# The modulation's matrix-vector products in a two-block network: all accumulation on VectorE, with weight buffers of their own

## The chip, the cores and the metric

The kernel is one program on one core of a Trainium2 chip. The metric is the device time of one execution in microseconds (us). Engines are named as in the profile: PE (TensorE, matrix products), DVE (VectorE), ACT (ScalarE), POOL (GpSimd), SP (SyncE, which here issues the weight loads).

## The reference

Two blocks of two layers each on 256 tokens of width 1024. The first block is FFN, a mixer of three attention kinds, FFN. The second block is conditioned: each of its two layers takes six rows of 1024 numbers from a modulation, for two conditions (the latent's and the context's), and shifts, scales and gates with them. Cut to what matters here:

```python
# c, c_ctx: the conditions' vectors [1024]; ada_w: [layers, 1024, 6 * 1024]
mod     = silu(c)     @ ada_w[i] + ada_b[i]    # six rows of 1024: shift, scale, gate, twice
mod_ctx = silu(c_ctx) @ ada_w[i] + ada_b[i]
h = rms_norm(x) * (1 + scale) + shift           # ahead of each mixer and MLP
x = x + gate * f(h)
```

The products with `ada_w` are matrix-vector products: 25 MB of weights for each layer are read once and multiplied by two vectors. They depend on nothing that the first block computes, so they can run beside it.

## The kernel before, in words

**FFN.** `ffn` goes over the 2816 hidden columns in five chunks of 512 and one of 256. For each chunk two products of 256 tokens x 1024 are formed, gate and up (`gemm`); each takes four weight tiles of 128 x 1024 numbers. `wload` (L230) loads a tile to `wraw` by a DMA in SP's queue (L237), casts it to `whi` on ACT (L244) and forms `wlo = wraw - whi` on DVE (L245). PE multiplies with `whi` and `wlo` in three passes (L284 to L286). After the chunk ACT makes `sg`, DVE makes `av` (L466, twice: one for each token tile), PE transposes `av` (L470), and ACT and DVE split the result to `ahi` and `alo` (L472, L473). Then the down product runs over 22 tiles in two halves, and DVE adds it to `x` (`residual`, L443); PE transposes `x` (L363) and DVE makes the low part of the next layer's input (L372).

**Buffers.** `wtile` (L219) hands out weight buffers in turn: four `wraw` of the program and three more in an FFN (`FFN_MORE`), four `whi` and four `wlo` in an FFN.

**The modulation.** `ada` (L969) is background work. For a group of 1024 columns it goes over eight tiles of 128 rows. A step takes the next `wraw` of the same ring that the FFN's tiles use, issues its load on SP (L982), and adds tile times `c` to an accumulator: for the first condition on DVE in one instruction (L991; L993 for the first tile); for the second condition ACT scales the tile into a buffer (L987) and POOL adds this to the second accumulator (L989). After eight steps PE sums over the partitions (L1001) and POOL writes the result to DRAM. The buffers, two accumulators and two for the scaled tile, lie in one tile `hB` (L1546); in the second block's MLP they are `xA0` and `xA1`. There are twelve groups: six of the first layer and two of the second for both conditions, beside the first block's FFNs; four of the second layer for one condition alone, beside the MLP of both conditions.

**What sets the order.** `background` (L196) takes a list of steps and spreads them over so many weight tiles; `tick` runs a step after each tile (T1 to T4 say over how many). That is the order in the code. The order on each engine is then made by a scheduler: it places an instruction when what it waits for is there in its own reckoning, and of several ready ones the one that comes first in the code. An engine runs its instructions strictly in that order, and SP's queue too.

Of the kernel before, what the change touches and what calls it, by code (L numbers as in the profile page):

```python
# [13 lines left out]
AF = mybir.ActivationFunctionType  # L14
# [6 lines left out]
S = 256  # L21
# [7 lines left out]
# background work: steps of the hyena filter, and how many of them go ahead of the modulation's  # L29
HY, W2 = 14, 4  # L30
# column chunk after which the bias strips are made
CB = 4
# after a gated output product (by token tiles): engines of the next weight tiles' parts (1: lo on GpSimd, 2: hi too)
ENG = {2: [0, 1], 4: [0, 1, 1]}
# weight tiles over which background work is spread, and to wait before
T1, T2, T3, T4 = 40, 54, 28, 36
W1, W3, W4 = 0, 4, 8
# columns of a gated output product's second half (by token tiles)
# [5 lines left out]
def consts():  # L44
    """Arrays that depend on shapes alone."""
# [19 lines left out]
    # second block: local attention's band, rope tables  # L65
# [15 lines left out]
    # retention decay: exponents and masks  # L81
# [5 lines left out]
    # long convolution: odd-frequency transform of length 512, filter features  # L87
# [12 lines left out]
class Net:  # L100
# [95 lines left out]
    def background(self, steps, tiles=1, wait=0):  # L196
        """Steps to run beside the next products, spread evenly over so many weight tiles, after some to wait."""
        self.fill, self.rate = steps, len(steps) / tiles
        self.credit = -wait * self.rate

    def tick(self):
        """After each weight tile: now and then a step of background work."""
        self.credit += self.rate
        while self.fill and self.credit >= 1.0:
            self.credit -= 1.0
            self.fill.pop(0)()
# [12 lines left out]
    def wtile(self, name, shape):  # L219
        """A weight buffer: in turn one of the pool's and of those that a phase adds"""  # L220
# [28 lines left out]
    def tiles(self, src, nk, c0, cn):  # L249
        """Plan of a product's weight tiles: (first k tile, k tiles)"""  # L250
        step = 2 if cn > 256 else 4
        return [(k0, min(step, nk - k0)) for k0 in range(0, nk, step)]

    def gemm(self, lhs, nk, src, c0, cn, nt, k_base=0, mid=None, done=None, skew=(False, False), turn=0):
        """Natural form: one accumulator [tok, cn] per token tile. skew: over the first / last weight
        tiles, the first token tiles go ahead of the last. turn: so many k tiles go last."""
# [35 lines left out]
    def gemm_t(self, hT, nk, src, c0, cn, tok, skew=False, whole=False):  # L292
        """Transposed form: accumulators [128 columns, tok] for cn / 128 column tiles. skew: over the
        first weight tiles, the first half of the tokens goes ahead of the second."""
# [10 lines left out]
        while i < len(plan):  # L305
# [14 lines left out]
            for (kt, wh, wl), c, q in order:  # L320
# [3 lines left out]
                # a bank's first product clears it; the first ones of its other parts then overwrite  # L324
# [7 lines left out]
    def rstd(self, ss, n, inv_n, out=None):  # L332
        """(ss / n + eps) ** -0.5"""
# [7 lines left out]
    def row_stats(self, x, ss, i, nt=2, c0=0, cn=512):  # L341
        """Sums of squares of columns c0 .. c0 + cn to ss[:, t, i]"""
# [5 lines left out]
    def row_rstd(self, ss):  # L348
        """rsqrt of the rows' mean squares, from sums of squares of parts [128, t, parts]"""
# [5 lines left out]
    def split_T(self, x, h, w, hi, lo):  # L355
        """hi, lo parts of (x * w)^T, [d, kt, tok], for half h of the columns"""
# [18 lines left out]
    def prep(self, x, w):  # L375
        """Rows' norm: raw rows times the gain, transposed, half by half; their rsqrt at the end."""
# [15 lines left out]
    def prep_mod(self, x, m, tok, kind, xA):  # L392
        """norm(x) * (1 + scale) + shift, transposed: raw rows times the gain half by half; the rest at the end."""
# [55 lines left out]
    def ffn(self, x, pre, wg, wu, wd, nxt, hook):  # L449
        """pre: this layer's rows, ready; nxt: makes the next layer's; hook: other work, after the first columns"""  # L450
# [33 lines left out]
    def bias_strips(self):  # L484
        """R[h, i] = bias of head h at distance 255 - i (or masked), 128 times in DRAM: strip[p, j] = R[h, j - p + 127]."""
# [17 lines left out]
    def strip(self, pool, h0):  # L503
        """Bias of four heads: [tok p, head, j], of distance p + 128 - j."""
# [6 lines left out]
    def head_stats(self, mp, src, n, r):  # L511
        """r[:, t, :n] = rsqrt(mean square) of the n heads in src [128, 2, n * 64]"""
# [11 lines left out]
    def nat(self, mp, w, c0, cn, lhs, r, name):  # L524
        """Columns c0 .. c0 + cn of norm(x) @ w_in, [tok, t, cn]"""
# [7 lines left out]
    def normed_q(self, mp, src, n, gain, name):  # L533
        """q heads (n, natural) -> normalized, transposed [128 (2 heads, d), n / 2, tok]"""
# [15 lines left out]
    def normed_k(self, mp, src, name):  # L550
        """two key heads -> normalized, each twice: [tok, t, g, 2, 64]"""
# [10 lines left out]
    def put_halves(self, dst0, dst1, ps, gain):  # L562
        """upper partitions to dst0, lower to dst1, times gain"""
# [11 lines left out]
    def mixer_tiles(self):  # L575
        """Keys and stick queries, transposed (a head in both halves of the partitions); the merged branches"""
# [11 lines left out]
    def compress(self, mp, kv1, l, out):  # L588
        """Compressed keys into self.KC; compressed values [(g, n) 32, 64] to out. Returns its steps."""
# [16 lines left out]
        # column groups of the array: (parity of j, key or value)  # L606
# [50 lines left out]
    def key_tiles(self, kd, dst, gain):  # L657
        """kd [tok, t, g, 2, 64] -> dst(g) [(2, 64), keys]"""
# [15 lines left out]
    def nsa(self, mp, t, g, qT, strip, sc, vs, vw, vc, gates, yhi, ylo):  # L674
# [5 lines left out]
        # the two heads of a pair: at the same time in the array's row halves, to different banks  # L680
# [66 lines left out]
        # the heads' parities: at the same time in the array's column halves  # L747
# [84 lines left out]
    def softmax_sink(self, S, rows, sink):  # L832
        """exponentials of S in place; returns 1 / (their sums + the sink's)"""
# [120 lines left out]
    def ada_setup(self):  # L954
# [7 lines left out]
        # to sum over the partitions, to row tok  # L962
# [6 lines left out]
    def ada(self, i, grps, bufs):  # L969
        """Columns g * 1024 .. + 1024 of the modulation of layer i, for both conditions, to DRAM, step by step.  # L970
        bufs: makes four buffers [128, 1024]. Of the last layer, the context's mixer takes two kinds only."""
# [4 lines left out]
        def step(g, kt):  # L976
            toks = (0, 1) if i == 0 or g < 2 else (0,)
            if not st:
                st["bufs"] = bufs()
            acc = st["bufs"][0:2]  # L980
            raw = self.wtile("wraw", [128, 1024])
            nc.sync.dma_start(raw, w[kt * 128:kt * 128 + 128, g * 1024:g * 1024 + 1024])  # L982
            for tok in toks:
                c = self.cT[:, tok * 8 + kt:tok * 8 + kt + 1]
                if tok:
                    y = st["bufs"][2 + kt % 2] if kt else acc[1]
                    nc.scalar.activation(y, raw, AF.Copy, scale=c)  # L987
                    if kt:
                        nc.gpsimd.tensor_add(acc[1], acc[1], y)  # L989
                elif kt:  # L990
                    nc.vector.scalar_tensor_tensor(acc[0], raw, c, acc[0], op0=ALU.mult, op1=ALU.add)  # L991
                else:
                    nc.vector.tensor_scalar(acc[0], raw, c, None, op0=ALU.mult)  # L993
            if kt < 7:
                return
            # sums over the partitions: the four column groups at the same time
# [10 lines left out]
        return [lambda g=g, kt=kt: step(g, kt) for g in grps for kt in range(8)]  # L1007

    def mod_columns(self, i):
        """[128 d, tok, kind, kt] of the modulation of layer i, scales with the norms' gains folded in"""  # L1010
# [31 lines left out]
    def sine(self, pool, arg):  # L1042
        """sin(arg) in place, reduced to [-pi, pi] first"""
# [13 lines left out]
    def hyena_filter(self):  # L1057
        """Transform of the filter (with the skip term folded in as lag 0, before its norm) to DRAM; 1 / norm. Step by step."""
# [68 lines left out]
    def even(self, x, ctx, hT, m, new_hT):  # L1127
# [4 lines left out]
        with tc.tile_pool(name="even", bufs=1) as ep:  # L1132
# [6 lines left out]
            # attention: projections, rotations, transposes  # L1139
# [41 lines left out]
            def attend(t):  # L1181
# [4 lines left out]
                for i in range(4):  # L1186
# [37 lines left out]
                    # the pair's heads: at the same time in the array's column halves  # L1224
# [6 lines left out]
            # long convolution  # L1231
# [376 lines left out]
```

## Time and profile before

| | |
|---|---|
| median of 3 runs | 2518.71 us (2515.84 to 2521.52) |
| profiled execution, span | 2524.6 us |
| PE busy | 2430.4 us, 96% |
| DVE busy | 1568.2 us, 62% |
| ACT busy | 1162.0 us, 46% |
| POOL busy | 308.0 us, 12% |
| adds of L989 on POOL | 56 of 2.96 us |

The span runs from the first to the last instruction of one profiled execution; no other time of that execution is recorded, and it lies 0.2% above the median of the runs. Busy shares are averages over stages. A wait belongs to the engine that stood idle, and names the instruction that ended it. PEclk is the clock that TensorE was granted, as a share of its full speed.

### The profile page before, as it was taken

The numbers are of one execution on the slowest core, as the hardware profiler recorded it, in microseconds if no ns is written. First come the engines' busy times: TensorE is split into PE (matmuls) and PEld (weight loads), VectorE is DVE, ScalarE is ACT, GpSimd is POOL, SyncE is SP. The second block draws the span as 40 slices with busy tenths as digits, with TensorE's granted clock in tenths as the row PEclk, the third lists the DMA queues.
The fourth block names the chain that finished last, engine by engine and source line by source line (L and its number), as shares of the span: only waits on it lengthen the run. The fifth ranks groups of instructions, "written<-read, shape, count | busy, mean of one in ns | idle before, by whom it ended". The sixth has DMA issues, their size and how long they took to land. (4 is left out here: it accounts for less than half of the span.)

```text
span 2524.6 us, 31452 instructions
## 1 busy us (share of the span) xinstructions
PE 2430.4 (96%) x11941; PEld 1933.3 (77%) x11941; DVE 1568.2 (62%) x2181; ACT 1162.0 (46%) x1771; POOL 308.0 (12%) x229
## 2 busy tenths in 40 slices
PE   8899999999998999999899999999999999998998
PEld 7777777777777877787687667777787788887996
DVE  5775576676677457767754674654534745655665
ACT  5544655555544455556443342431333433334543
POOL 2330100133123001003300000100000110110000
PEclk9999999999999999999899999999999999999999
DMA  7685545767666564466743121455522433334553
GB/s 245 214 261 171 176 124 159 234 195 228 214 202 208 157 192 148 133 208 202 226 160 117 51 101 50 129 180 177 160 100 84 136 92 111 112 119 150 183 185 133
DMA packets 212351, 405.86 MB, mean 161 GB/s; under 512 B 14830, under 2 KB 48365, under 8 KB 211688
## 3 DMA queue, kind: packets, MB, share of 16 engines
q1 hardware_dynamic: 207416, 391.77, 49.3%
q0 software_dynamic: 3776, 9.38, 1.1%
q10 hardware_dynamic: 1008, 2.70, 0.3%
q8 instruction: 94, 1.54, 0.2%
q14 instruction: 57, 0.47, 0.1%
HBM read 401.48 MB, written 4.67 MB: 161 GB/s over the span
## 5 line engine op out<-in xcount | busy, mean ns | idle before, releaser
L245 DVE TENSOR_TENSOR wlo<-wraw,whi 128x1024 fp32r<-128x1024 f32 (+1 forms) x617 | 812.9, 1324 | 593.7 <-ACT whi L244 589.8
L244 ACT CAST whi<-wraw 128x1024 fp32r<-128x1024 f32 (+1 forms) x622 | 646.4, 1044 | 893.3 <-PE acc L286 666.4
L284 PE MATMUL acc<-whi,hA 128*128 128x512 f32 (+1 forms) x1472 | 570.2, 388 | 1.4 <-ACT whi L244 1.0
L285 PE MATMUL acc<-wlo,hA 128*128 128x512 f32 (+1 forms) x1472 | 566.4, 385 | 3.4 <-DVE wlo L245 3.4
L286 PE MATMUL acc<-whi,hA 128*128 128x512 f32 (+2 forms) x1152 | 441.0, 383 | 0.0
L284 PEld LDWEIGHTS acc<-whi,hA 128*128 128x128 f32 x1472 | 281.0, 191 | 67.4 <-issue 9.3
L285 PEld LDWEIGHTS acc<-wlo,hA 128*128 128x128 f32 x1472 | 280.5, 191 | 60.1 <-DVE wlo L245 7.0
L284 PE MATMUL acc<-whi,ahi 128*128 128x512 f32 x736 | 293.3, 399 | 0.0
L285 PE MATMUL acc<-wlo,ahi 128*128 128x512 f32 x736 | 291.4, 396 | 1.5 <-DVE wlo L245 1.5
L286 PE MATMUL acc<-whi,alo 128*128 128x512 f32 x736 | 291.2, 396 | 0.0
L326 PE MATMUL acc<-hA,whi 128*128 128x512 f32 (+1 forms) x752 | 259.0, 345 | 3.7 <-ACT hA L425 3.0
L327 PE MATMUL acc<-hA,wlo 128*128 128x512 f32 (+1 forms) x752 | 258.4, 344 | 2.4 <-POOL wlo L245 2.4
L328 PE MATMUL acc<-hB,whi 128*128 128x512 f32 (+1 forms) x752 | 257.4, 344 | 0.0
L286 PEld LDWEIGHTS acc<-whi,hA 128*128 128x128 f32 x1152 | 220.5, 191 | 42.7 <-issue 1.3
L989 POOL TENSOR_TENSOR hB<-hB 128x1024 f32<-128x1024 f32 x56 | 165.7, 2959 | 326.9 <-ACT hB L987 308.7
L285 PEld LDWEIGHTS acc<-wlo,ahi 128*128 128x128 f32 x736 | 138.6, 188 | 34.7 <-DVE wlo L245 2.9
L284 PEld LDWEIGHTS acc<-whi,ahi 128*128 128x128 f32 x736 | 138.6, 188 | 34.3 <-issue 2.1
L286 PEld LDWEIGHTS acc<-whi,alo 128*128 128x128 f32 x736 | 138.5, 188 | 32.9
L326 PEld LDWEIGHTS acc<-hA,whi 128*128 128x128 f32 x752 | 142.3, 189 | 24.9 <-ACT hA L425 3.5
L327 PEld LDWEIGHTS acc<-hA,wlo 128*128 128x128 f32 x752 | 142.5, 189 | 23.6 <-issue 3.4
L328 PEld LDWEIGHTS acc<-hB,whi 128*128 128x128 f32 x752 | 142.1, 189 | 19.3 <-issue 1.4
L991 DVE SCALAR_TENSOR_TENSOR hB<-wraw,cT,hB 128x1024 f32<-128x1024 f32 x56 | 98.6, 1760 | 43.9 <-DMA wraw<-in_ada_w_dram 43.7
(422 smaller groups left out, 2745.9 us busy)
## 6 DMA issues: line engine op xcount, KB each, us to landing
wraw<-in_mlp_w_dram SPq DMA_DIRECT2D x128, 512.0 KB, 3.8
wraw<-in_ada_w_dram SPq DMA_DIRECT2D x96, 512.0 KB, 4.0
wraw<-in_ffn_w_gate_dram SPq DMA_DIRECT2D x88, 512.0 KB, 4.3
wraw<-in_ffn_w_up_dram SPq DMA_DIRECT2D x88, 512.0 KB, 4.5
wraw<-in_ffn_w_down_dram SPq DMA_DIRECT2D x88, 512.0 KB, 3.7
wraw<-in_w_in_dram SPq DMA_DIRECT2D x84, 512.0 KB, 3.7
wraw<-in_od_w_in_dram SPq DMA_DIRECT2D x64, 512.0 KB, 3.7
wraw<-in_ev_w_in_dram SPq DMA_DIRECT2D x18, 512.0 KB, 3.7
```

Source lines behind the costliest of these rows:

```text
L244: nc.scalar.copy(hi[sl], raw[sl])
L245: (nc.gpsimd if e & 1 else nc.vector).tensor_sub(lo[sl], raw[sl], hi[sl].bitcast(F32))
L284: nc.tensor.matmul(o, h, wh, start=kt == first, stop=False)
L285: nc.tensor.matmul(o, h, wl, start=False, stop=False)
L286: nc.tensor.matmul(o, l, wh, start=False, stop=kt == end)
L326: nc.tensor.matmul(o, wh[:, cs], xh[:, kt, ts], start=st, stop=False, skip_group_check=skew_or_pair)
L327: nc.tensor.matmul(o, wl[:, cs], xh[:, kt, ts], start=False, stop=False, skip_group_check=skew_or_pair)
L328: nc.tensor.matmul(o, wh[:, cs], xl[:, kt, ts], start=False, stop=en, skip_group_check=skew_or_pair)
L989: nc.gpsimd.tensor_add(acc[1], acc[1], y)
L991: nc.vector.scalar_tensor_tensor(acc[0], raw, c, acc[0], op0=ALU.mult, op1=ALU.add)
```

## The change

`ada` is written anew. Both conditions are accumulated on DVE, one instruction each (L992 in the new numbering; the first tile of the second condition stays with ACT, L994). POOL adds nothing. The weights no longer come through the ring of `wraw`: the two buffers that held scaled tiles are now two weight buffers in turn, in the same tile `hB` (or `xA1`), and a step first issues the load for the step after it (L980). A new first step makes the buffers and issues the first load, so a phase has one step more. T1, the number of weight tiles over which two of the five phases are spread, goes from 40 to 46. The rest of the diff takes away comments.

```diff
-T1, T2, T3, T4 = 40, 54, 28, 36
+T1, T2, T3, T4 = 46, 54, 28, 36
...
-        def step(g, kt):
+        todo = [(g, kt) for g in grps for kt in range(8)]
+
+        def load(n):
+            g, kt = todo[n]
+            nc.sync.dma_start(st["bufs"][2 + n % 2], w[kt * 128:kt * 128 + 128, g * 1024:g * 1024 + 1024])
+
+        def step(n):
+            g, kt = todo[n]
             toks = (0, 1) if i == 0 or g < 2 else (0,)
-            if not st:
-                st["bufs"] = bufs()
             acc = st["bufs"][0:2]
-            raw = self.wtile("wraw", [128, 1024])
-            nc.sync.dma_start(raw, w[kt * 128:kt * 128 + 128, g * 1024:g * 1024 + 1024])
+            if n + 1 < len(todo):
+                load(n + 1)
+            raw = st["bufs"][2 + n % 2]
             for tok in toks:
                 c = self.cT[:, tok * 8 + kt:tok * 8 + kt + 1]
-                if tok:
-                    y = st["bufs"][2 + kt % 2] if kt else acc[1]
-                    nc.scalar.activation(y, raw, AF.Copy, scale=c)
-                    if kt:
-                        nc.gpsimd.tensor_add(acc[1], acc[1], y)
-                elif kt:
-                    nc.vector.scalar_tensor_tensor(acc[0], raw, c, acc[0], op0=ALU.mult, op1=ALU.add)
+                if kt:
+                    nc.vector.scalar_tensor_tensor(acc[tok], raw, c, acc[tok], op0=ALU.mult, op1=ALU.add)
+                elif tok:
+                    nc.scalar.activation(acc[1], raw, AF.Copy, scale=c)
                 else:
                     nc.vector.tensor_scalar(acc[0], raw, c, None, op0=ALU.mult)
...
-        return [lambda g=g, kt=kt: step(g, kt) for g in grps for kt in range(8)]
+        def first():
+            st["bufs"] = bufs()
+            load(0)
+
+        return [first] + [lambda n=n: step(n) for n in range(len(todo))]
```

**First place: DVE in the second layer's first FFN, up to the `av` of its fifth chunk.** Before, an `av` pair is preceded by tiles' `wlo` and one accumulation for every one or two of them:

```order
L993 TENSOR_SCALAR hB_5771<-wraw_6238,cT_543 128x1024
L245 TENSOR_TENSOR wlo_6234<-wraw_6232,whi_6233 128x1024
L991 SCALAR_TENSOR_TENSOR hB_5771<-wraw_6302,cT_543,hB_5771 128x1024
L245 TENSOR_TENSOR wlo_6256<-wraw_6254,whi_6255 128x1024
L991 SCALAR_TENSOR_TENSOR hB_5771<-wraw_6361,cT_543,hB_5771 128x1024
L245 TENSOR_TENSOR wlo_6298<-wraw_6296,whi_6297 128x1024
L991 SCALAR_TENSOR_TENSOR hB_5771<-wraw_6404,cT_543,hB_5771 128x1024
L245 TENSOR_TENSOR wlo_6321<-wraw_6319,whi_6320 128x1024
L245 TENSOR_TENSOR wlo_6339<-wraw_6337,whi_6338 128x1024
L466 SCALAR_TENSOR_TENSOR av_6274<-acc_6194,rs_5547,sg_6272 128x512
```

Now the densest chunk reads, in its later part:

```order
L992 SCALAR_TENSOR_TENSOR hB_5711<-hB_5711,cT_543 128x1024 x2
L245 TENSOR_TENSOR wlo_6354<-wraw_6352,whi_6353 128x1024
L992 SCALAR_TENSOR_TENSOR hB_5711<-hB_5711,cT_543 128x1024
L245 TENSOR_TENSOR wlo_6396<-wraw_6394,whi_6395 128x1024
L992 SCALAR_TENSOR_TENSOR hB_5711<-hB_5711,cT_543 128x1024
L245 TENSOR_TENSOR wlo_6429<-wraw_6427,whi_6428 128x1024
L992 SCALAR_TENSOR_TENSOR hB_5711<-hB_5711,cT_543 128x1024 x2
L466 SCALAR_TENSOR_TENSOR av_6372<-acc_6293,rs_5487,sg_6370 128x512
```

Between this `av` and the pair before it stand ten accumulations (L992), one first product (L996) and seven `wlo`, where four or so accumulations stood.

**Second place: SP in the first FFN.** Before, every second or third load of an FFN tile is followed by one of the modulation, into the same ring:

```order
L982 DMA wraw_596<-in_ada_w_2_dram 128x1024
L237 DMA wraw_612<-in_ffn1_w_gate_dram 128x2x512
L237 DMA wraw_632<-in_ffn1_w_up_dram 128x2x512
L982 DMA wraw_638<-in_ada_w_2_dram 128x1024
L237 DMA wraw_655<-in_ffn1_w_up_dram 128x2x512
L237 DMA wraw_673<-in_ffn1_w_up_dram 128x2x512
L237 DMA wraw_691<-in_ffn1_w_up_dram 128x2x512
L982 DMA wraw_697<-in_ada_w_2_dram 128x1024
```

Now they go to `hB`:

```order
L237 DMA wraw_788<-in_ffn1_w_gate_dram 128x2x512
L980 DMA hB_595<-in_ada_w_2_dram 128x1024 x2
L237 DMA wraw_808<-in_ffn1_w_up_dram 128x2x512
L237 DMA wraw_826<-in_ffn1_w_up_dram 128x2x512
L980 DMA hB_595<-in_ada_w_2_dram 128x1024
L237 DMA wraw_847<-in_ffn1_w_up_dram 128x2x512
L237 DMA wraw_865<-in_ffn1_w_up_dram 128x2x512
L980 DMA hB_595<-in_ada_w_2_dram 128x1024
```

The loads of steps three and four stand together behind the FFN tiles that were loaded ahead, and each waits for the accumulations that free its buffer.

**Third place: DVE at the end of the first mixer.** Before, the residual sums and the low parts stand among `wlo` alone:

```order
L443 SCALAR_TENSOR_TENSOR x_75<-acc_3673,x_75 128x512
L443 SCALAR_TENSOR_TENSOR x_75<-acc_3674,x_75 128x512
L245 TENSOR_TENSOR wlo_3829<-wraw_3827,whi_3828 128x1024
L245 TENSOR_TENSOR wlo_3891<-wraw_3889,whi_3890 128x1024
L372 SCALAR_TENSOR_TENSOR hA_3671<-tp_3787,vaT_532,hA_3671 128x256
L372 SCALAR_TENSOR_TENSOR hA_3671<-tp_3796,vaT_532,hA_3671 128x256
```

Now:

```order
L992 SCALAR_TENSOR_TENSOR hB_4240<-hB_4240,cT_543 128x1024 x2
L443 SCALAR_TENSOR_TENSOR x_75<-acc_3643,x_75 128x512
L443 SCALAR_TENSOR_TENSOR x_75<-acc_3644,x_75 128x512
L245 TENSOR_TENSOR wlo_3781<-wraw_3779,whi_3780 128x1024
L245 TENSOR_TENSOR wlo_3799<-wraw_3797,whi_3798 128x1024
L992 SCALAR_TENSOR_TENSOR hB_4240<-hB_4240,cT_543 128x1024
L245 TENSOR_TENSOR wlo_3861<-wraw_3859,whi_3860 128x1024
L992 SCALAR_TENSOR_TENSOR hB_4240<-hB_4240,cT_543 128x1024
L372 SCALAR_TENSOR_TENSOR hA_3641<-tp_3757,vaT_532,hA_3641 128x256
L372 SCALAR_TENSOR_TENSOR hA_3641<-tp_3766,vaT_532,hA_3641 128x256
```

The next phase's first steps have moved ahead of its FFN, into the mixer's last product. The same holds at the end of the other mixer and of the first layer's last FFN.

## Rows read from the trace of the kernel before

**Rows 1.** The page, part 1: busy us, share of the span, instructions.

```profile
span 2524.6 us, 31452 instructions
## 1 busy us (share of the span) xinstructions
PE 2430.4 (96%) x11941; PEld 1933.3 (77%) x11941; DVE 1568.2 (62%) x2181; ACT 1162.0 (46%) x1771; POOL 308.0 (12%) x229
```

**Rows 2.** Waits of PE: who waited for whom, us in total, times, longest.

```profile
PE tp L470 <- DVE av L466: 42.2, 12, 7.9
...
PE acc L285 <- DVE wlo L245: 4.9, 4, 1.8
```

**Rows 3.** Stretches: length, busy us per engine, PEclk, DMA share, GB/s.

```profile
62.00:166.00 104.00, 94.08 (x459) 76.39 (x458) 77.54 (x64) 54.87 (x63) 38.80 (x16) 0.95 0.74 238
474.00:648.00 174.00, 170.43 (x796) 132.43 (x795) 132.10 (x126) 92.22 (x109) 49.27 (x21) 1.00 0.68 214
648.00:816.00 168.00, 151.36 (x682) 121.65 (x681) 118.00 (x96) 84.48 (x98) 44.19 (x19) 0.94 0.66 207
1146.00:1266.00 120.00, 103.05 (x470) 81.41 (x468) 92.06 (x70) 63.17 (x75) 44.66 (x18) 0.91 0.67 214
1600.00:1830.00 230.00, 229.31 (x1003) 181.87 (x1002) 126.57 (x138) 69.34 (x92) 7.48 (x13) 1.00 0.54 172
```

**Rows 4.** Timeline 1222 to 1252: start, us, instruction, [idle before, what ended it].

```profile
1221.87 13.20 POOL L989 TENSOR_TENSOR hB<-hB 128x1024 f32<-128x1024 f32 x4
...
1226.16 6.70 DVE L245 TENSOR_TENSOR wlo<-wraw,whi 128x1024 fp32r<-128x1024 f32 x2
...
1232.79 3.36 DVE L991 SCALAR_TENSOR_TENSOR hB<-wraw,cT,hB 128x1024 f32<-128x1024 f32 x1
...
1238.00 1.12 PE L470 MATMUL tp<-k_ident,av 128*128 128x128 f32 x4 [7.88 <-DVE av L466]
```

**Rows 5.** DVE's groups, 28 to 60, no modulation: busy, mean ns, idle before.

```profile
L245 DVE TENSOR_TENSOR wlo<-wraw,whi 128x1024 fp32r<-128x1024 f32 x12 | 14.7, 1225 | 15.8 <-ACT whi L244 15.8
L466 DVE SCALAR_TENSOR_TENSOR av<-acc,rs,sg 128x512 f32<-128x512 f32 x4 | 2.8, 743 | 0.0
L473 DVE TENSOR_TENSOR alo<-tp,ahi 128x512 fp32r<-128x512 f32 x2 | 1.3, 680 | 0.0
```

**Rows 6.** DVE's groups, 1600 to 1830, the MLP of both conditions.

```profile
L991 DVE SCALAR_TENSOR_TENSOR xA<-wraw,cT,xA 128x1024 f32<-128x1024 f32 x28 | 35.9, 1284 | 47.9 <-DMA wraw<-in_ada_w_dram 47.4 <-DVE wlo L245 0.4
```

**Rows 7.** DVE's groups, 1146 to 1266, the last FFN's first part.

```profile
L245 DVE TENSOR_TENSOR wlo<-wraw,whi 128x1024 fp32r<-128x1024 f32 x33 | 52.7, 1610 | 21.3 <-ACT whi L244 21.3
L991 DVE SCALAR_TENSOR_TENSOR hB<-wraw,cT,hB 128x1024 f32<-128x1024 f32 x14 | 30.0, 2144 | 4.0 <-DMA wraw<-in_ada_w_dram 3.9
L466 DVE SCALAR_TENSOR_TENSOR av<-acc,rs,sg 128x512 f32<-128x512 f32 x8 | 5.7, 740 | 0.9 <-PE acc L286 0.9
```

**Rows 8.** Two stalls and what follows, PE alone: length, busy, PEclk, DMA.

```profile
691.50:695.00 3.50, 0.00 (x0) 0.88 0.78 279
695.00:701.00 6.00, 5.94 (x18) 0.50 0.67 181
...
1230.10:1238.00 7.90, 0.02 (x2) 0.50 0.53 154
1238.00:1243.80 5.80, 5.80 (x18) 0.51 0.78 241
```

**Rows 9.** Line L987: ns min/median/max, first and last start.

```profile
L987 ACT ACTIVATE hB<-wraw,cT x64: 1134/1154/1166, 65.2 to 1247.8; 128x1024 f32<-128x1024 f32 x64
```

**Rows 10.** Timeline 27 to 62, PE: the first transposes of two chunks.

```profile
35.49 0.66 PE L470 MATMUL tp<-k_ident,av 128*128 128x128 f32 x4
...
58.72 0.66 PE L470 MATMUL tp<-k_ident,av 128*128 128x128 f32 x4
```

**Rows 11.** Line L982, the modulation's loads: from issue to landing.

```profile
DMA to landing us min/median/max: 3.6/4.0/10.6
```

## The prediction

> **What bounds the kernel now.** I read the page's busy shares first, then PE's waits, then a table of stretches, then the timeline of one stall. PE is busy 2430.4 of 2524.6 us [rows 1], so the end is set by PE, and only what stops or slows PE is to be had. Its one large wait is for the transposes of `av` (L470), which wait for VectorE's L466: 42.2 us in 12 waits; with 4.9 us more for `wlo` (L245) that is 47.1 us [rows 2]. The table of stretches [rows 3] says where. Its first four stretches are the FFN stages in which the modulation of both conditions runs: PE idles 9.9, 3.6, 16.6 and 17.0 us there (length less busy), 47.1 us together, the same sum again. The fifth is the two-condition MLP, where the modulation runs for one condition almost throughout and GpSimd adds nothing: PE idles 0.7 us. In that stretch VectorE's accumulations wait 47.4 us for their loads [rows 6] and it costs nothing.
>
> The timeline shows what a stall is made of [rows 4]. Around 1222 to 1236 GpSimd runs four adds (L989), 13.20 us; two `wlo` of VectorE take 6.70 us in that time and an accumulation (L991) takes 3.36 us. `av` stands behind them, and PE stands 7.88 us. In a stretch without the modulation a `wlo` takes 1.225 us and an `av`, which reads PSUM, 0.743 us [rows 5]; an accumulation takes 1.284 us where GpSimd does not add [rows 6]. In the last of the four stages the means are 1.610 and 2.144 us, while `av` stays at 0.740 [rows 7]. So VectorE's operations on SBUF stretch beside the adds.
>
> [...]
>
> **What the change removes.** (a) 56 adds on GpSimd (eight column groups of both conditions, seven each) and with them VectorE's stretching. In the stage 1146 to 1266: 14 x (2.144 - 1.284) + 33 x (1.610 - 1.225) = 12.0 + 12.7 = 24.7 us of VectorE [rows 6, 7], 1.8 us for each of 14 adds. (b) 56 scaled copies on ScalarE, 1.154 us each [rows 9], 65 us. ScalarE is busy 46% [rows 1], so by itself this moves nothing. (c) 96 turns in the ring of `wraw`: FFN weights keep all seven buffers, and a modulation load no longer waits for an FFN tile to be done with.
>
> **What it adds.** 56 accumulations on VectorE at 1.284 us, 72 us. In the stage 1146 to 1266 that is 14 x 1.284 = 18.0 us against the 24.7 us returned: VectorE falls from 92.1 to about 85 us. PE there has 103.1 us of work, some 96 at full clock. VectorE remains below PE, at 89%. T1 from 40 to 46 only spreads steps of two phases; I cost it at nothing.
>
> The order shows that steps do not spread evenly: the loads depend no longer on the ring, so eight steps of a column group come close together, then pause until their sums are formed. So the test is a chunk, from one pair of `av` to the next. PE's own time for one is 58.72 - 35.49 = 23.2 us [rows 10]. VectorE's densest chunk, the first place shown in the order, has ten accumulations and one first product (counted alike): 11 x 1.284 = 14.1; seven `wlo`, 8.6; two `av` and two `alo`, 2.8; together 25.6 us, 2.3 too many [rows 5, 6]. The first chunk of the first FFN has eight and one, seven `wlo`: 23.0 us; the next six and nine: 21.6 us. Both fit. Only two chunks are of the densest kind (the other is in the last FFN), and VectorE enters one with a lead, since between two `wlo` it now idles 1.3 us on average for ScalarE [rows 5]. Bounds for each 0 and 2.3; I take 1.5, 3 us for both. At ten other chunk ends an accumulation may just be running as `av` falls due: 0 to 1.28 each; I take 0.5, 5 us. For the lower clock behind what is left, 1.5 us.
>
> **Loads and queues.** A load is issued by SP a step ahead, but only when the step before has freed the buffer, and takes 4.0 us (median) to land [rows 11]. A step of two accumulations and one `wlo` takes 3.8 us, so a load is late by 0.2 us there and by 1.4 us where no `wlo` stands between. SP is in order: behind a waiting modulation load stand FFN loads (second place of the order), but these have seven buffers; with eight tiles to a chunk that is 20 us of PE's work ahead. Cost 0.
>
> **Boundaries.** The third place of the order: the first steps of three phases now go in the end of the stage before, ahead of the residual sums (L443) and low parts (L372) on VectorE that PE's transposes and next products wait for. No row of before has this. Each boundary can lose nothing, or two accumulations, 2.6 us [rows 6]; gains are excluded, as nothing is taken away there. I take 1 us each, 3 us: the order puts them where VectorE had been idle.
>
> **The MLP** of two conditions changes its buffers alone: 0.7 us of idle, no change.
>
> **Sum.** Idle removed 47.1. Missing clock in the four stages, (1 - clock) x length, is 5.2 + 0 + 10.1 + 10.8 = 26.1 us [rows 3]; part of it lies under idle already counted. In the two stalls of [rows 8] the part under work is 2.8 of 6.8 and 3.0 of 3.4 us, 42% and 88%: 11 to 23 us, I take 17. Against it 3 + 5 + 1.5 + 3 = 12.5. Net 51.6 us. The profiled execution, 2524.6 us, would become 2473. It lies 5.9 us above the median of the runs, 2518.7; on that scale I predict 2467 us. The bounds: with nothing left over and the clock's 23 us, 70 us, 2449; with the upper ends of the bounds here (4.6 + 12.8 + 3 + 7.7) and the clock's 11 us, 30 us, 2489.
>
> **Rivals.** *Loads late (14%).* The change does not do what it says: loads are a step ahead in the program, but the bunched steps run faster than loads land. Eight column groups, some 2.5 steps in each with no `wlo` between, 1.4 us: 28 us of VectorE's waiting, just ahead of `av`. Net 23 us, 2495. For it: VectorE waits for these loads in every stage now [rows 6]. Against it: most steps in the order have a `wlo` between.
>
> *No difference (5%).* The late loads, and every upper end above besides, 4.6 + 12.8 + 3 + 7.7 = 28 us, with the clock's lower bound: 47.1 + 11 - 28 - 28 = 2 us, 2517.
>
> *VectorE becomes the bound (9%).* The stretching isn't GpSimd's but comes with a full VectorE beside loads; then no 1.8 us returns per add, and the 56 accumulations cost what they cost in the stages now. At 2.144 and 1.610 us [rows 7] the densest chunk takes 11 x 2.144 + 7 x 1.610 + 2.8 = 37.7 us against 23.2, 14 too many; an average chunk of a group, with half the excess, 7. With 2 us of clock behind each, and some ten such chunks, about 92 us come against 64 taken away: 28 slower, 2547. It decides from 6.4 us for each of ten chunks. Against it: 1.284 us is the mean of 28 accumulations in the MLP, beside the same kind of loads at 172 GB/s [rows 3, 6], and `av` does not stretch at all [rows 7].
> [...]
>
> **How the numbers follow.** My forecast has 72%, and its own range is 2449 to 2489. The range of 8 in 10 is 2450 to 2496: above it lie half of the first rival, the second and the third, 19% or so, below it little. Measurement tells 0.2%, 5 us, from no change. Faster 0.86: forecast and first rival; same 0.05; slower 0.09.
>
> **What would show it.** In the profile after: no adds on GpSimd; 140 accumulations (84 and 56) of 1.28 us and `wlo` near 1.23 us in the FFN stages; the wait of L470 for L466 below 10 us; PE idle in the four stages below 15 us; the granted clock at 1.00 in most of them. Wrong would be: accumulations near 1.8 us (third rival), waits of VectorE for loads into `hB` above 25 us just ahead of `av` (first), or new waits of PE for L443 and L372 above 8 us (boundaries).

## The result, and the profile after

The changed kernel takes 2478.66 us (median; 2474.79 to 2480.61) where the kernel before, timed beside it, takes 2520.11 us (2515.84 to 2526.86): a ratio of 0.9826, 95% interval 0.9810 to 0.9842. It is faster by 1.7%, 41 us. The forecast was 2467 us with a range of 2450 to 2496. The profiled execution of the kernel after has a span of 2473.0 us, against 2524.6 us before.

The engines' busy times [rows 1] first. PE is now busy for 98% of the span; GpSimd's busy time has fallen from 308.0 to 143.1 us and ScalarE's from 1162.0 to 1106.6. VectorE, which has taken over 56 accumulations, is busy for *less* than before, 1541.5 instead of 1568.2 us.

```profile
PE 2412.0 (98%) x11941; PEld 1919.4 (78%) x11941; DVE 1541.5 (62%) x2237; ACT 1106.6 (45%) x1715; POOL 143.1 (6%) x173
```

PE's waits [rows 2], as engine, line waited for, total us, times and longest. The wait of the transposes for `av` has gone from 42.2 to 8.4 us, that for `wlo` from 4.9 to 0.7. Two have come up: the wait for `rl` (L1378, at the start of the MLP), 3.1 us where before had 0.7, shown last, and 1.5 us for `hA` (L372), at a stage's boundary.

```profile
PE tp L470 <- DVE av L466: 8.4, 7, 3.9
...
PE acc L326 <- ACT rl L1378: 3.1, 1, 3.1
...
PE acc L286 <- DVE hA L372: 1.5, 1, 1.5
...
PE acc L285 <- DVE wlo L245: 0.7, 2, 0.5
```

```profile
PE acc L326 <- ACT rl L1371: 0.7, 1, 0.7
```

The stretches [rows 3] at the same times (stretch, its length, busy us of each engine with counts, granted clock, DMA share, GB/s). In the four FFN stretches PE idles 2.1, 0.0, 2.1 and 0.0 us, where it idled 9.9, 3.6, 16.6 and 17.0, and the granted clock is 1.00 in each (0.95, 1.00, 0.94 and 0.91 before). The work lies up to 50 us earlier now, so a stretch doesn't hold the same work to the last tile, and the gap of 4.0 us at 466, shown below, lies just outside them.

```profile
62.00:166.00 104.00, 101.91 (x509) 83.10 (x508) 81.41 (x81) 47.16 (x55) 2.31 (x4) 1.00 0.78 255
474.00:648.00 174.00, 174.00 (x821) 135.76 (x821) 111.20 (x124) 77.45 (x93) 9.81 (x9) 1.00 0.59 186
648.00:816.00 168.00, 165.90 (x797) 135.04 (x796) 120.11 (x120) 77.84 (x92) 3.10 (x3) 1.00 0.74 233
1146.00:1266.00 120.00, 120.00 (x606) 98.00 (x605) 82.27 (x86) 58.31 (x77) 2.34 (x4) 1.00 0.62 197
```

VectorE's groups in the last of these stretches [rows 7] (busy us, mean ns of one, idle time ahead and what ended it). The rows of weight halves are back at 1.221 us (1.610 before), the accumulations at 1.277 us (2.144 before), and `av` stands where it always stood.

```profile
L245 DVE TENSOR_TENSOR wlo<-wraw,whi 128x1024 fp32r<-128x1024 f32 x41 | 50.0, 1221 | 35.6 <-ACT whi L244 35.6
L992 DVE SCALAR_TENSOR_TENSOR hB<-hB,cT 128x1024 f32<-128x1024 f32 x14 | 17.5, 1277 | 1.5 <-DMA hB<-in_ada_w_dram 1.5
L466 DVE SCALAR_TENSOR_TENSOR av<-acc,rs,sg 128x512 f32<-128x512 f32 x6 | 4.4, 744 | 0.6 <-PE acc L286 0.6
```

What is left has two main places. The longest wait for `av`, 3.9 us, is in the first chunk of the second FFN of layer 0. On VectorE's timeline (start, us, line, operation, idle time ahead) two accumulations stand between the last `wlo` rows and the `av` that PE waits for:

```profile
464.75 1.28 DVE L992 SCALAR_TENSOR_TENSOR hB<-hB,cT 128x1024 f32<-128x1024 f32 x1 [0.49 <-DMA hB<-in_ada_w_dram]
465.95 1.22 DVE L245 TENSOR_TENSOR wlo<-wraw,whi 128x1024 fp32r<-128x1024 f32 x1
467.08 1.28 DVE L992 SCALAR_TENSOR_TENSOR hB<-hB,cT 128x1024 f32<-128x1024 f32 x1
468.28 1.22 DVE L245 TENSOR_TENSOR wlo<-wraw,whi 128x1024 fp32r<-128x1024 f32 x1
469.42 1.40 DVE L466 SCALAR_TENSOR_TENSOR av<-acc,rs,sg 128x512 f32<-128x512 f32 x2
```

The other is the start of the MLP. VectorE stands 4.11 us in front of an accumulation whose weights haven't landed in `xA`; `alo` (L672) and `sq` (L1380) stand behind it, ScalarE waits for those before it can make the next `rl`, and PE waits for `rl`:

```profile
1550.12 0.68 DVE L1380 TENSOR_TENSOR sq<-rl 128x512 f32<-128x512 f32 x1
1554.91 1.28 DVE L992 SCALAR_TENSOR_TENSOR xA<-xA,cT,xA 128x1024 f32<-128x1024 f32 x1 [4.11 <-DMA xA<-in_ada_w_dram]
1556.11 0.68 DVE L672 TENSOR_TENSOR alo<-sq,ahi 128x512 fp32r<-128x512 f32 x1
1556.71 1.28 DVE L1380 TENSOR_TENSOR sq<-rl 128x512 f32<-128x512 f32 x2
```

### The profile page after: what moved, and what is told of

Same layout as the page of the kernel before. It is cut to its first block, busy times and chain, and to the rows that moved or that the text cites. A ratio compares the mean times of both kernels' runs of the same rounds, so it can differ in the third digit from the quotient of the medians.

```text
span 2473.0 us, 31296 instructions
## 1 busy us (share of the span) xinstructions
PE 2412.0 (98%) x11941; PEld 1919.4 (78%) x11941; DVE 1541.5 (62%) x2237; ACT 1106.6 (45%) x1715; POOL 143.1 (6%) x173
## 5 line engine op out<-in xcount | busy, mean ns | idle before, releaser
L245 DVE TENSOR_TENSOR wlo<-wraw,whi 128x1024 fp32r<-128x1024 f32 (+1 forms) x617 | 750.5, 1220 | 609.0 <-ACT whi L244 604.2
L286 PE MATMUL acc<-whi,hA 128*128 128x512 f32 (+2 forms) x1152 | 435.8, 378 | 1.5 <-DVE hA L372 1.5
L284 PEld LDWEIGHTS acc<-whi,hA 128*128 128x128 f32 x1472 | 277.3, 188 | 65.6 <-issue 8.6
L286 PEld LDWEIGHTS acc<-whi,hA 128*128 128x128 f32 x1152 | 217.0, 188 | 44.4 <-DVE hA L372 2.1
L286 PEld LDWEIGHTS acc<-whi,alo 128*128 128x128 f32 x736 | 138.3, 188 | 33.2 <-issue 0.4
L992 DVE SCALAR_TENSOR_TENSOR hB<-hB,cT 128x1024 f32<-128x1024 f32 x112 | 141.0, 1278 | 21.6 <-DMA hB<-in_ada_w_dram 21.3
L286 PE MATMUL acc<-whi,hB 128*128 128x512 f32 (+1 forms) x320 | 123.0, 387 | 2.4 <-DVE hB L426 2.3
```

The costliest lines, as they stand in the source:

```text
L245: (nc.gpsimd if e & 1 else nc.vector).tensor_sub(lo[sl], raw[sl], hi[sl].bitcast(F32))
L284: nc.tensor.matmul(o, h, wh, start=kt == first, stop=False)
L286: nc.tensor.matmul(o, l, wh, start=False, stop=kt == end)
L992: nc.vector.scalar_tensor_tensor(acc[tok], raw, c, acc[tok], op0=ALU.mult, op1=ALU.add)
```

## The experiments

Two theories stood against each other. **C**: the adds on GpSimd hold up VectorE's operations on SBUF, and the gain is their removal. **L**: the modulation's loads in the shared ring of weight buffers hold back the FFN's weights, and the gain is the own buffers. Beside them, that a full VectorE is the limit (**D**). In the experiments the line of the accumulation shifts a little (L986 to L995).

**The kernel before, once more (e0).** No edit.

> The kernel before once more, nothing changed, for a second profiled execution. The first one has a span of 2524.6 us, the longest of its runs (2515.8 to 2526.9), and the one of the kernel after, 2473.0, is the shortest of its runs (2474.8 to 2480.6): the profiles differ by 51.6 us, the medians by 41.5. If that gap of 10 us is spread between executions, this profile comes out at a span of 2514 to 2520 with waits of the transposes of line 470 for av that sum to 33 to 39 us instead of 42.2, and with fewer of the 6.8 us stretches at half clock. If it is not, the span is again about 2524 and those waits again about 42 us.

Measured: 2521.64 us (median, 2517.39 to 2525.30), and the profiled execution has a span of 2515.6 us. PE's waits for `av` sum to 36.0 us, those for `wlo` to 5.4, and four FFN stretches that begin as much earlier as the work does here show this:

```profile
PE tp L470 <- DVE av L466: 36.0, 13, 7.9
...
PE acc L285 <- DVE wlo L245: 5.4, 5, 2.9
```

```profile
60.00:164.00 104.00, 94.91 (x462) 77.03 (x461) 78.42 (x65) 55.18 (x63) 38.74 (x16) 0.95 0.74 240
472.00:646.00 174.00, 170.40 (x796) 132.61 (x795) 132.88 (x126) 91.95 (x109) 49.25 (x21) 1.00 0.66 214
646.00:814.00 168.00, 156.15 (x728) 125.99 (x727) 118.24 (x98) 87.15 (x101) 44.83 (x19) 0.95 0.66 213
1137.00:1257.00 120.00, 103.57 (x477) 82.26 (x476) 92.36 (x71) 63.48 (x75) 43.86 (x18) 0.94 0.67 213
```

PE idles 41.0 us in the four (104.00 - 94.91 and so on), not 47.1, and the clock's missing part, (1 - clock) x length, is 20.8 us, not 26.1. So two executions of one and the same program differ by 9.0 us of span, and these stalls and the clock behind them are most of it. The profile on which the prediction rests was a long one; this one is the shortest of its ten timed runs, so neither is typical.

**One part alone: no GpSimd, loads still in the ring (e1).** In the kernel before:

```
-                if tok:
-                    y = st["bufs"][2 + kt % 2] if kt else acc[1]
-                    nc.scalar.activation(y, raw, AF.Copy, scale=c)
-                    if kt:
-                        nc.gpsimd.tensor_add(acc[1], acc[1], y)
-                elif kt:
-                    nc.vector.scalar_tensor_tensor(acc[0], raw, c, acc[0], op0=ALU.mult, op1=ALU.add)
+                if kt:
+                    nc.vector.scalar_tensor_tensor(acc[tok], raw, c, acc[tok], op0=ALU.mult, op1=ALU.add)
+                elif tok:
+                    nc.scalar.activation(acc[1], raw, AF.Copy, scale=c)
```

> The kernel before with one part of the change: the second condition is accumulated on VectorE, no scaled copies on ScalarE and no adds on GpSimd; the loads still go through the shared ring of weight buffers, in their own step, and the steps are spread over 40 weight tiles. Theory C (the 3 us adds on GpSimd stretch VectorE's work on SBUF, and the chain load, scale, add is late): the gain is here already, 2476 to 2490 us, accumulations at about 1.28 us, weight rows (wlo) at about 1.22. Theory L (the loads in the shared ring hold back the weight tiles behind them): still 2505 to 2518, with waits for loads ahead of the weight halves. Theory D (VectorE full): no gain either, with waits of the transposes for av above 40 us.

Measured: 2468.13 us (2463.62 to 2473.69), ratio to before 0.9799 (0.9780 to 0.9819). The whole gain is there, and the median is 8 us below the range that C gave and 10.5 us below the kernel after (the intervals of the two ratios still overlap; e8, e3 and e4 below settle it). C holds, L and D fall. Its accumulations take 1.279 us and the transposes wait 5.5 us for `av`:

```profile
L986 DVE SCALAR_TENSOR_TENSOR hB<-wraw,cT,hB 128x1024 f32<-128x1024 f32 x112 | 141.0, 1279 | 35.6 <-DMA wraw<-in_ada_w_dram 35.5
```

```profile
PE tp L470 <- DVE av L466: 5.5, 7, 1.3
```

**The other part alone: own buffers, GpSimd as before (e2).** In the kernel after:

```
+                if kt and tok:
+                    nc.scalar.activation(raw, raw, AF.Copy, scale=c)
+                    nc.gpsimd.tensor_add(acc[1], acc[1], raw)
+                elif kt:
-                if kt:
-                    nc.vector.scalar_tensor_tensor(acc[tok], raw, c, acc[tok], op0=ALU.mult, op1=ALU.add)
+                    nc.vector.scalar_tensor_tensor(acc[0], raw, c, acc[0], op0=ALU.mult, op1=ALU.add)
```

> The kernel after with the other part alone: own buffers and loads a step ahead stay, but the second condition is scaled on ScalarE again (in place, after VectorE has read the tile) and added on GpSimd. Theory C: most of the gain is lost, 2500 to 2525 us, wlo rows of 1.5 to 2.4 us beside the adds, accumulations of the first condition at 1.7 to 2.2 us, waits of the transposes for av of 25 to 45 us. Theory L: the gain stays, 2474 to 2490 us.

Measured: 2536.31 us (2533.16 to 2540.13), ratio 1.0069 (1.0051 to 1.0088): slower than the kernel before, and worse than C said. The accumulations of the first condition take 1.736 us, and a wait has come up that neither the kernel before nor the kernel after has, 11.8 us at the stages' ends for the residual sums (L443), ahead of which accumulations of the next phase and stretched `wlo` now stand:

```profile
L995 DVE SCALAR_TENSOR_TENSOR hB<-hB,cT 128x1024 f32<-128x1024 f32 x56 | 97.2, 1736 | 41.5 <-DMA hB<-in_ada_w_dram 41.3
```

```profile
PE tp L470 <- DVE av L466: 28.0, 9, 8.4
...
PE tp L363 <- DVE x L443: 11.8, 3, 6.0
```

The four kernels make a square (medians, us):

| second condition | loads in the ring | own buffers |
|---|---|---|
| on ScalarE and GpSimd | 2520.1 (before) | 2536.3 (e2) |
| on VectorE | 2468.1 (e1) | 2478.7 (after) |

Taking GpSimd out is worth 52 or 58 us; the own buffers *cost* 10 or 16 (7 or 17 by the ratios to the kernel before, timed beside each). (In e2 a buffer comes free only after GpSimd's add, and the 56 accumulations wait 41.3 us for their loads, where the 112 of the kernel after wait 21.3.)

**Adds that nobody waits for (e5).** In the kernel after, behind each accumulation of the second condition:

```
+                    if tok:
+                        scr = self.ffp.tile([128, 768], F32, name="scr", bufs=1)
+                        nc.gpsimd.tensor_add(scr, raw[:, 0:768], raw[:, 0:768])
+                        nc.gpsimd.tensor_add(scr[:, 0:256], raw[:, 768:1024], raw[:, 768:1024])
```

> The kernel after with adds on GpSimd put beside the accumulations whose result nobody reads: for each step of the second condition two adds of the loaded tile to itself, 768 and 256 columns, into a scratch tile. Nothing waits for them but the next load into that buffer, so no result is late through them. Theory C, in the form that the adds slow VectorE down by being there: wlo and the accumulations stretch to 1.5 to 2.4 us in these stages, and the time is 2500 to 2540 us. If the loss of the kernel before came from the order of the chain (a result of GpSimd or of ScalarE coming late) and not from the stretch: 2474 to 2485 us.

Measured: 2524.98 us (2521.24 to 2527.94), ratio 1.0015 (1.0004 to 1.0026). Useless adds give back the whole gain. No result is late through them, and the accumulations' waits for loads, 13.2 us, are fewer than the 21.3 of the kernel after; it is the durations that grow, 1.629 us for an accumulation in the FFN stages against 1.278. The timeline shows how:

```profile
478.49 1.29 DVE L992 SCALAR_TENSOR_TENSOR hB<-hB,cT 128x1024 f32<-128x1024 f32 x1 [1.02 <-DMA hB<-in_ada_w_dram]
478.60 2.50 POOL L995 TENSOR_TENSOR scr<-hB 128x768 f32<-128x768 f32 x1 [10.62 <-DMA hB<-in_ada_w_dram]
479.69 2.49 DVE L245 TENSOR_TENSOR wlo<-wraw,whi 128x1024 fp32r<-128x1024 f32 x1
481.18 1.48 POOL L996 TENSOR_TENSOR scr<-hB 128x256 f32<-128x256 f32 x1
482.11 4.03 DVE L992 SCALAR_TENSOR_TENSOR hB<-hB,cT 128x1024 f32<-128x1024 f32 x2
482.73 2.32 POOL L995 TENSOR_TENSOR scr<-hB 128x768 f32<-128x768 f32 x1
485.14 1.48 POOL L996 TENSOR_TENSOR scr<-hB 128x256 f32<-128x256 f32 x1
486.06 0.74 DVE L466 SCALAR_TENSOR_TENSOR av<-acc,rs,sg 128x512 f32<-128x512 f32 x1
```

Here the engines take turns. The `wlo` that began at 479.69 ends at 482.18, 1.08 us after GpSimd's add of 478.60 has ended (481.10), a little less than the length that it has alone (1.22 us); the add behind ends about half a microsecond after that `wlo`. The first accumulation, which began 0.11 us before the add, takes its 1.29 us, and `av`, one of whose inputs is in PSUM, takes its 0.74.

**Fills and copies in place of the adds (e11, e12).** The same place, two other operations:

```
+                        nc.gpsimd.tensor_copy(scr[:, 0:1], raw[:, 0:1])
+                        for _ in range(4):
+                            nc.gpsimd.memset(scr, 0.0)
```

> The kernel after with work on GpSimd that writes SBUF and reads none, in the place of e5's adds: a copy of one column of the loaded tile (that ties it to the step) and then four fills of 768 columns with zero. If VectorE is held up by GpSimd's reads: accumulations stay at 1.28 us, and the time at 2474 to 2484 us. If any work of GpSimd on SBUF holds it up: accumulations of 1.5 us and more, 2500 to 2525 us.

```
+                        nc.gpsimd.tensor_copy(scr, raw[:, 0:768])
+                        nc.gpsimd.tensor_copy(scr, raw[:, 256:1024])
```

> The kernel after with reads on GpSimd that have one input instead of two, in the place of e5's adds: two copies of 768 columns of the loaded tile to scratch per step. If any read of GpSimd holds VectorE up: accumulations of 1.5 us and more, and 2495 to 2525 us. If it takes two inputs: 2474 to 2484 us, accumulations at 1.28.

Measured: with the fills 2480.09 us (2478.41 to 2482.54), the time of the kernel after; with the copies 2512.22 us (2504.11 to 2520.54), ratio to before 0.9955 (0.9939 to 0.9972). The fills keep GpSimd busy for 166.0 us and the copies for 161.2, so it isn't GpSimd's being busy that counts. With fills the 112 accumulations of the FFN stages take 1.279 us, with copies 1.516 (with the adds of e5 1.629). First two rows of e11, then three of e12:

```profile
L997 POOL MEMSET scr<- 128x768 f32 x224 | 166.0, 741 | 13.0
...
L992 DVE SCALAR_TENSOR_TENSOR hB<-hB,cT 128x1024 f32<-128x1024 f32 x112 | 141.2, 1279 | 27.9 <-DMA hB<-in_ada_w_dram 27.6 <-ACT hB L999 0.3
```

```profile
L992 DVE SCALAR_TENSOR_TENSOR hB<-hB,cT 128x1024 f32<-128x1024 f32 x112 | 167.5, 1516 | 13.8 <-DMA hB<-in_ada_w_dram 13.5 <-ACT hB L998 0.3
L996 POOL COPY scr<-hB 128x768 f32<-128x768 f32 x56 | 88.1, 1574 | 3.5
L995 POOL COPY scr<-hB 128x768 f32<-128x768 f32 x56 | 73.1, 1306 | 343.0 <-DMA hB<-in_ada_w_dram 209.1 <-PE acc L286 133.3
```

So in these runs VectorE's accumulations are longer beside GpSimd's reads of SBUF, with two inputs (e5, 1.629 us) or one (e12, 1.516), and beside fills, which only write, they aren't (e11, 1.279; 1.278 in the kernel after).

**ScalarE's copies kept (e10).** The kernel before with one word changed:

```
-                        nc.gpsimd.tensor_add(acc[1], acc[1], y)
+                        nc.vector.tensor_add(acc[1], acc[1], y)
```

> The kernel before with one word changed: the adds of the second condition run on VectorE instead of GpSimd; the scaled copies stay on ScalarE, the loads in the ring. If taking GpSimd out is the whole gain and the 65 us of ScalarE's copies moved nothing: 2465 to 2474 us, as e1. If relieving ScalarE is a part of the gain: 2476 to 2490.

Measured: 2473.73 us (2473.00 to 2475.84), ratio 0.9809 (0.9788 to 0.9830). With ScalarE's 56 copies back in place nearly all of the gain stays. Whether the 5.6 us to e1 are the copies can't be told: the intervals of the two ratios overlap.

**What the own buffers cost (e8, e3, e4).** Three edits apart: e1 with the wider spread (T1 from 40 to 46), the kernel after with the narrower one (T1 from 46 to 40), and the kernel after with each load in its own step:

```
-            if n + 1 < len(todo):
-                load(n + 1)
+            load(n)
...
-            load(0)
```

> The kernel of e1 (before, both conditions on VectorE, loads in the shared ring) with one number more of the change: the first two phases spread over 46 weight tiles instead of 40. Theory B (the own buffers, loaded a step ahead, cost the 10 us by which the kernel after is behind e1, since they let the steps bunch and run ahead into the stages' ends): 2465 to 2472 us, as e1. Theory S (the wider spread costs them): 2474 to 2482.

> The kernel after with the spread of before, 40 weight tiles instead of 46. Theory B (own buffers cost the 10 us): no change, 2474 to 2483 us. Theory S (the spread costs them): 2465 to 2472.

> The kernel after with each load issued in its own step instead of the one before; the two own buffers stay. If issuing ahead is what holds SP's queue or lets the steps bunch: 2466 to 2473 us. If the buffers alone set when a load can start (a load waits for its buffer's last reader whenever it is issued): 2475 to 2483, with the same waits of PE as the kernel after. If loads come late without the lead: 2484 to 2500, with waits of VectorE for loads into hB well above the 21 us of the kernel after.

Measured: e8 2470.32 us (2468.16 to 2472.41), e3 2479.54 (2477.81 to 2483.07), e4 2477.65 (2474.69 to 2479.67). The spread moves nothing, and neither does the lead: without it the accumulations in `hB` wait 22.5 us for loads, with it 21.3. What separates the groups is the buffers alone: all eight timed runs of e1 and e8 lie at or below 2473.7 us, all twelve of after, e3 and e4 at or above 2474.7.

**Where they cost it (e7, e9).** The kernel after with the MLP's loads through the ring again (e7), and with those of the second FFN of layer 0 too (e9, with `grps[0] == 2` alone as the condition; both leave out the load ahead there):

```
             raw = st["bufs"][2 + n % 2]
+            if grps[0] == 2 and i:
+                raw = self.wtile("wraw", [128, 1024])
+                nc.sync.dma_start(raw, w[kt * 128:kt * 128 + 128, g * 1024:g * 1024 + 1024])
```

> The kernel after with the MLP's share of the modulation (28 accumulations) loaded through the shared ring again, as before; the FFN stages keep their own buffers. Theory B, place MLP: there an accumulation stood at VectorE's head 4.1 us for its load while PE waited 3.1 us for the first squares behind it, and 3.4 us at half clock followed; both go, and the time is 2472 to 2477 us, 4 to 5 below the kernel after. If the wait comes from elsewhere: no change, 2476 to 2482.

> The kernel after with two phases loaded through the shared ring again, the MLP's (as e7) and that of the second FFN of the first layer; the others keep their own buffers. Theory B, place two: in that FFN two accumulations stand ahead of the first av and PE waits 4.0 us for it in the kernel after, 4.4 in e7, against 1.2 in e1; 3.4 to 6.8 us at half clock follow. Both go: 2467 to 2471 us, level with e1, and the bunched steps are the whole of the difference between e1 and the kernel after. If the rest is spread over the other boundaries: no change against e7, 2472 to 2477.

Measured: e7 2473.94 us (2469.60 to 2477.39), ratio 0.9811 (0.9791 to 0.9831). PE's wait for `rl`, 3.1 us in the kernel after, is down to 0.2 us, and the time is 4.7 us lower, as expected for this place; the interval of the ratio still overlaps that of the kernel after, so the mechanism is shown by the traces (the wait is 2.4 to 3.7 us in the profiles of the seven kernels whose MLP has own buffers, 0.2 to 1.6 us in the seven that load through the ring, e0 among them) and the size only roughly by the times. e9 fails its expectation: 2476.47 us (2474.39 to 2477.57), no gain on e7. The wait at 466 is down to 1.2 us as forecast, but later in the same FFN a load through the ring comes 4.07 us late in front of an `av`:

```profile
538.28 2.36 DVE L245 TENSOR_TENSOR wlo<-wraw,whi 128x1024 fp32r<-128x1024 f32 x2
544.70 1.28 DVE L995 SCALAR_TENSOR_TENSOR hB<-wraw,cT,hB 128x1024 f32<-128x1024 f32 x1 [4.07 <-DMA wraw<-in_ada_w_dram]
545.90 0.74 DVE L466 SCALAR_TENSOR_TENSOR av<-acc,rs,sg 128x512 f32<-128x512 f32 x1
```

PE waits 4.2 us there. So either way of loading can put a late load ahead of an `av`; where it falls is a matter of the order. The wait at 466 does go with the own buffers, 3.5 to 4.4 us in after, e3, e4, e7 and e11, 1.2 in e1, e8, e9 and e10; but e9 gains nothing by its going, since the other wait has come up. Some 5 us of the difference between e1 and the kernel after stay without a place that an experiment shows.

## Why the prediction was right, and where it was off

**The cause** held: VectorE's accumulations stretch beside adds on GpSimd whose results nobody reads (e5, 1.629 us against 1.278) and beside copies (e12, 1.516), not beside fills (e11, 1.279), and without the adds the gain comes with the loads in the ring too (e1, 2468.1 us). The 1.277 us of an accumulation in the FFN stages is the 1.284 that the MLP's row gave [rows 6].

**ScalarE's copies**, costed at nothing: 5.6 us by the medians of e10 and e1, and not told apart from none.

**What is left over** was put at 12.5 us. Waits for `av` and `wlo`: 8 forecast, 9.1 found (8.4 + 0.7), but in other places. The two densest chunks (ten accumulations, seven or eight `wlo`) end with `av` at 775 and 1206 us: PE waits 1.4 us at the first and nothing worth listing at the second, where 1.5 each were forecast. The largest rest, 3.9 us, stands at the end of a first chunk with few steps: there the `whi` of its last tiles, and with them `wlo`, come late behind a load that ScalarE waits for (4.76 us ahead of L1088), so VectorE has no lead and each accumulation ahead of `av` counts. In e1 ScalarE waits 4.61 us for the same load, no accumulation stands ahead of that `av`, and PE waits 1.2 us. Clock: 1.5 forecast; behind that rest PE works 3.2 us at a granted clock of 0.50, 1.6 us lost. Boundaries: 3 forecast, 1.5 found, one of three (L372).

**The MLP** was costed at no change, from the row that VectorE waits 47.4 us for loads there and PE idles 0.7 us. That is the step that failed by mechanism: own buffers changed *which* accumulation waits. The one at the MLP's start now waits ahead of the `alo` and `sq` that ScalarE and PE need, 3.1 us instead of 0.7, and 3.4 us at half clock follow: some 4 us. "Loads and queues, cost 0" fell with it, and (c), that the FFN's weights keep all seven buffers, brought no net gain. Own buffers as a whole cost 7 to 10 us where GpSimd is out, as the square shows; the prediction had 3 for the boundaries and 3 for the two chunks of bunched steps.

**The size.** On the profile's own scale the sum came out to the microsecond, 51.6 us from 2524.6 to 2473, and this agreement is partly chance. PE's idle time, span less busy, fell by 33.2 us (94.2 to 61.0), where the sum has 36.1 (47.1 less 8 and 3); PE's busy time, with the same number of instructions, fell by 18.4 us, where the sum has 15.5 of clock (17 less 1.5). The two errors of 2.9 us cancel. The clock's term itself was well taken: in the four stages 34.7 us of PE's work lie in stretches with a granted clock of 0.50, which is 17.3 us lost.

The step that was mis-sized is the last one, taking the 51.6 us from the median of 2518.7 as well; from the kernel before to the kernel after the median fell by 41.5. In the runs that have both, the time is 1.8 to 2.0 us above the span, so the profiled execution before stands for some 2526.4 us, 7.7 above that median, and the one after, the shortest of its four, lies 3.9 below theirs: together nearly all of the 11.7 us by which the forecast is low. The stalls themselves are a large part of what makes the one execution longer than the other (spans of 2524.6 and 2515.6 us, with 47.1 and 41.0 us of PE's idle time in the four stages), so the long one holds more of them to remove. By the rows of e0 the same sum is 41.4 us of waits for `av` and `wlo`, 16.3 us of clock (32.7 us of work at 0.50 to 0.51), less 12.5: 45.2 us. That is from the shortest of ten executions; a typical one lies between the two, and how much of the gap to the measured 41.5 is the own buffers and how much the draw of executions stays open.

**The rivals.** Loads late: a place or two, 4 us at the MLP, not 28; the waits into `hB` are 21.3 us in all and mostly hidden. No difference: out, at 41 us faster. VectorE as the bound: out, since the accumulations in the FFN stages return to 1.28 us with VectorE busy for 81.4 of 104 us.

## What to carry to other kernels

In this kernel, where VectorE's `wlo` and accumulations stand a few microseconds ahead of what PE waits for, work on GpSimd that reads SBUF wasn't free even when nobody needed its result: with such adds the time was 2525.0 us (e5) and with copies 2512.2 (e12), against 2478.7 without and 2480.1 with fills (e11). In another kernel compare the same VectorE operation beside GpSimd's work and away from it, and move the work to VectorE if it costs less there than it stretches. When a gain is the removal of stalls, size it from more than one execution: here the longer of two held 47.1 us of PE's idle time in the four stages and the shorter 41.0, and the sum from the longer couldn't be taken from the median. And test the parts of a change apart, since one can carry the gain and another, the own buffers here, take some back: the fastest version found is e1, the accumulations on VectorE alone, at 2468 us.

## What the chip showed that was not expected

That the two engines take turns here: the `wlo` of e5 shown above, 1.22 us long away from the adds, takes 2.49 beside them, ending 1.08 us after the add has ended. In e5 94 of 140 accumulations take 1.27 to 1.29 us and 45 of the other 46 take 1.6 and more; and all 85 accumulations and `wlo` that take over 1.32 us beside an add end 1.08 to 1.09 us after an add has ended; so do all 52 of the kernel before (39 `wlo`, 13 accumulations). And that fills do nothing of the kind: beside 224 fills of 741 ns each no accumulation of e11 took more than 1.294 us.
